# A row softmax that streams its data in equal chunks, and the same softmax on an in-place ring with a row maximum and chunks of unequal size

## The chip, the core and the metric

The kernel runs on one core of one Trainium2 chip. The core has engines that each work through their own list of instructions in order and meet through semaphores: VectorE (DVE in the profile), ScalarE (ACT), GpSimd (POOL), TensorE (PE, unused here) and SyncE (SP). Sixteen DMA engines move data between main memory and the on-chip memory; transfers are issued from the queues of SP and ACT (SPq and ACTq in the profile). The metric is the device time of one execution in microseconds. The kernel before has a median of 163.53 us over five runs (163.46 to 163.77).

## The reference: what is computed

The input has shape 16 x 1024 x 512 in float32, which is 16,384 rows of 512 numbers, 33.55 MB. Each row becomes its softmax:

```
x_max = np.max(x, axis=-1, keepdims=True)
exp_x = np.exp(x - x_max)
return (exp_x / np.sum(exp_x, axis=-1, keepdims=True)).astype(np.float32)
```

The subtraction of the row maximum cancels in the quotient. The inputs are drawn from a standard normal distribution, so an exponential without that subtraction stays small.

## The kernel before, in words

The 16,384 rows are seen as 16 chunks. One chunk has 128 partitions with R = 8 consecutive rows on each, so it is a block of 2 MB that lies together in main memory, and each partition reads or writes 16 KB of it in one piece. The loop over the chunks does the following for each.

- Load (line 47): SP issues one transfer into an `x_tile`. The pool of `x_tile` has seven buffers, so loads run far ahead of the work.
- Guard copy (line 49): GpSimd copies one column of the tile into a small tile. Nothing reads it; GpSimd just waits for each load this way. Four one-column memsets at line 80 do the same at the end for the last stores.
- Exponentials (line 61): ScalarE runs eight ACTIVATE instructions, one for each row position, from `x_tile` to `e_tile`, each 128 x 512. Each also adds up its row into a column of `sums`; that adding appears in the profile as an instruction of its own, ACTIVATION_READ_ACCUMULATOR. The row maximum is switched off (`use_max` is false), so the bias is the constant 0.
- Reciprocal (line 71) and scaling (line 74): VectorE inverts the eight sums and multiplies the whole 128 x 4096 tile by them in one TENSOR_TENSOR, in place in `e_tile`. There are four `e_tile` buffers.
- Store (line 76): ACT issues one 2 MB transfer to the output.

A scheduler orders each engine's list. On ACT it puts the sixteen exponentials of two chunks first, and then the two stores of these chunks. Completion of transfers is counted on eight semaphores, which the transfers take in turn in the order of the schedule. A transfer that takes a counter whose last user has not landed waits for it, so no more than eight transfers, loads and stores together, are under way.

The page calls a piece of a transfer that one DMA engine moves on its own a packet. Here it is the 16 KB of one partition, with small extra packets of 4 bytes that count completions.

Of the kernel before, what the change touches and what calls it, by code (L numbers as in the profile page):

```python
# [2 lines left out]

# [4 lines left out]


@with_exitstack  # L10
def kernel(
    ctx: ExitStack,
    tc: tile.TileContext,
    x: bass.AP,
    out: bass.AP,
):
    nc = tc.nc
    P = nc.NUM_PARTITIONS

    x_flat = x.flatten_outer_dims()  # L20
    out_flat = out.flatten_outer_dims()
    n, d = x_flat.shape

    R = int(os.environ.get("SM_R", "8"))
    XBUFS = int(os.environ.get("SM_XBUFS", "7"))
    EBUFS = int(os.environ.get("SM_EBUFS", "4"))

    rows_per_chunk = P * R
    assert n % rows_per_chunk == 0
    nchunks = n // rows_per_chunk  # L30

    x_t = x_flat.rearrange("(t p r) d -> t p r d", p=P, r=R)
    out_t = out_flat.rearrange("(t p r) d -> t p r d", p=P, r=R)

    x_pool = ctx.enter_context(tc.tile_pool(name="xp", bufs=XBUFS))
    e_pool = ctx.enter_context(tc.tile_pool(name="ep", bufs=EBUFS))
    stats_pool = ctx.enter_context(tc.tile_pool(name="stats", bufs=12))
    guard_pool = ctx.enter_context(tc.tile_pool(name="guard", bufs=1))

    use_max = os.environ.get("SM_USEMAX", "0") == "1"  # L40

    guard_tile = guard_pool.tile([P, 1], mybir.dt.float32)

    e_tiles = []
    for t in range(nchunks):
        x_tile = x_pool.tile([P, R, d], mybir.dt.float32)
        nc.sync.dma_start(out=x_tile, in_=x_t[t])  # L47

        nc.gpsimd.tensor_copy(out=guard_tile, in_=x_tile[:, 0, 0:1])  # L49

        if use_max:
            neg_max = stats_pool.tile([P, R], mybir.dt.float32)
            nc.vector.reduce_max(
                out=neg_max, in_=x_tile, axis=mybir.AxisListType.X, negate=True
            )

        e_tile = e_pool.tile([P, R, d], mybir.dt.float32)
        e_tiles.append(e_tile)
        sums = stats_pool.tile([P, R], mybir.dt.float32)
        for r in range(R):  # L60
            nc.scalar.activation(  # L61
                out=e_tile[:, r, :],
                in_=x_tile[:, r, :],
                func=mybir.ActivationFunctionType.Exp,
                bias=neg_max[:, r : r + 1] if use_max else 0.0,
                scale=1.0,
                accum_out=sums[:, r : r + 1],
            )

        recip = stats_pool.tile([P, R], mybir.dt.float32)  # L70
        nc.vector.reciprocal(out=recip, in_=sums)  # L71

        recip_b = recip.unsqueeze(2).to_broadcast([P, R, d])
        nc.vector.tensor_mul(out=e_tile, in0=e_tile, in1=recip_b)  # L74

        nc.scalar.dma_start(out=out_t[t], in_=e_tile)  # L76

    for b in range(min(EBUFS, nchunks)):
        e_tile = e_tiles[nchunks - 1 - b]
        nc.gpsimd.memset(e_tile[:, 0, 0:1], 0.0)  # L80


# [1 line left out]
_INS = ['x']  # L84
_OUTS = [((16, 1024, 512), 'float32')]


# [23 lines left out]
```

The softmax here doesn't subtract the row's maximum and nothing guards it: scores larger than these inputs give would overflow.

## Time and profile before

| What | Value |
|---|---|
| Median of five runs | 163.53 us |
| Profiled execution, its own time | 163.77 us |
| Its span | 161.8 us |
| VectorE busy | 74.1 us, 46% |
| ScalarE busy | 80.8 us, 50% |
| GpSimd busy | 13.5 us, 8% |
| Moved by DMA | 67.13 MB, mean 415 GB/s over the span |
| Data transfers | 16 loads and 16 stores of 2 MB |

The span runs from the first to the last instruction that the profile counts; the execution's own time is 2.0 us longer. Busy shares of engines are means over the span. The row of DMA digits on the page divides the span into 40 slices of 4.05 us and gives the mean busy share of the sixteen DMA engines in tenths. The GB/s row under it gives what they moved in the same slices. A view over chosen windows gives the same for any stretch of time; since a packet is counted where it begins, short windows swing around the true rate.

### The profile page before, as it was taken

How to read it: one execution, taken by the hardware profiler on the slowest of the kernel's cores; microseconds unless marked ns; L12 is line 12 of the kernel's file. 1: busy time of each engine (PE TensorE's matmuls, PEld its weight loads, DVE VectorE, ACT ScalarE, POOL GpSimd, SP SyncE). 2: the span in 40 equal slices, each digit the busy share in tenths (PEclk: the TensorE clock that was granted, in tenths of full speed). 3: DMA queues.
4: the chain of work that ended last, by engine and by line, in shares of the span. 5: the costliest groups of instructions: out<-in, count | busy, mean ns of one | idle time of the engine just before them, and what ended most of it. 6: DMA issues, size and time to landing. Idle time of an engine off the chain costs nothing.

```text
span 161.8 us, 456 instructions
## 1 busy us (share of the span) xinstructions
DVE 74.1 (46%) x32; ACT 80.8 (50%) x257; POOL 13.5 (8%) x24
## 2 busy tenths in 40 slices
DVE  0006960994296419082000008951992399069600
ACT  3099529924793381910000099339906980995000
POOL 0000000034080000000000006300000000000000
DMA  5999999999999999999999999999999999999993
GB/s 166 421 450 421 425 336 436 433 421 442 429 425 438 429 429 434 433 421 442 425 429 442 421 433 442 413 442 440 413 438 442 413 442 429 421 446 425 425 438 146
DMA packets 4610, 67.13 MB, mean 415 GB/s; under 512 B 512, under 2 KB 512, under 8 KB 512
## 3 DMA queue, kind: packets, MB, share of 16 engines
q1 hardware_dynamic: 2304, 33.56, 49.5%
q10 hardware_dynamic: 2304, 33.56, 48.5%
q14 instruction: 2, 0.02, 0.0%
HBM read 33.55 MB, written 33.55 MB: 415 GB/s over the span
## 4 chain that ended last, share of the span: by engine, by line
DMA 52%; ACT 28%; DVE 17%; issue 1%; ACTq 1%; POOLq 0%; SPq 0%
DMA x_tile<-in_x_dram 35%; ACT e_tile L61 28%; DMA out_dram<-e_tile 17%; DVE e_tile L74 16%; ACTq L76 1%; DVE recip L71 1%; POOLq L106 0%; POOLq L80 0%; SPq L47 0%
## 5 line engine op out<-in xcount | busy, mean ns | idle before, releaser
L61 ACT ACTIVATE e_tile<-x_tile 128x512 f32<-128x512 f32 x128 | 78.5, 615 | 66.3 <-DMA x_tile<-in_x_dram 35.2
L74 DVE TENSOR_TENSOR e_tile<-e_tile,recip 128x4096 f32<-128x4096 f32 x16 | 70.8, 4426 | 0.6
L71 DVE RECIPROCAL recip<-sums 128x8 f32<-128x8 f32 x16 | 3.2, 203 | 77.8 <-ACT e_tile L61 77.8
L61 ACT ACTIVATION_READ_ACCUMULATOR e_tile<-x_tile 128x1 f32 x128 | 23.9, 187 | 0.0
L49 POOL COPY guard_tile<-x_tile 128x1 f32<-128x1 f32 x16 | 12.9, 807 | 124.1 <-DMA x_tile<-in_x_dram 124.1
L80 POOL MEMSET e_tile<- 128x1 f32 x4 | 0.4, 99 | 23.1 <-DMA out_dram<-e_tile 23.1
L61 ACT ACT_TABLE_LOAD x1 | 1.3, 1283 | 0.7 <-PEq L95 0.7
L95 POOL MEMSET const-float32-0.0<- 128x1 f32 x1 | 0.1, 99 | 0.2 <-issue 0.2
L95 POOL MEMSET const-bfloat16-1.0<- 128x1 bf16 x1 | 0.1, 102 | 0.0
L95 POOL MEMSET const-uint8-127<- 128x1 uint8 x1 | 0.1, 102 | 0.0
L95 POOL MEMSET const-float32-1.0<- 128x1 f32 x1 | 0.1, 99 | 0.0
## 6 DMA issues: line engine op xcount, KB each, us to landing
x_tile<-in_x_dram SPq DMA_DIRECT2D x16, 2048.0 KB, 42.3
out_dram<-e_tile ACTq DMA_DIRECT2D x16, 2048.0 KB, 17.9
```

The lines of the kernel that those rows point to most:

```text
L49: nc.gpsimd.tensor_copy(out=guard_tile, in_=x_tile[:, 0, 0:1])
L61: nc.scalar.activation(out=e_tile[:, r, :], in_=x_tile[:, r, :], func=mybir.ActivationFunctionType.Exp, bias=neg_max[:, r : r + 1] if use_ ...
L71: nc.vector.reciprocal(out=recip, in_=sums)
L74: nc.vector.tensor_mul(out=e_tile, in0=e_tile, in1=recip_b)
L76: nc.scalar.dma_start(out=out_t[t], in_=e_tile)
L80: nc.gpsimd.memset(e_tile[:, 0, 0:1], 0.0)
L95: nc = _bacc.Bacc("TRN2", target_bir_lowering=False, num_devices=1)
```

## The change

The changed kernel keeps one launch, the same inputs and outputs, float32 everywhere, loads from SP and stores from ACT. It differs in these points.

- The chunks have 1, 1, 2, 4, 8, six times 16, 8, 4, 2, 1, 1 rows on each partition. That is again 16 chunks and 128 rows on each partition. The pieces that a partition moves are 2, 4, 8, 16 or 32 KB long, and a transfer has 256 KB to 4 MB.
- There is one ring of tiles. The exponentials write over the loaded data, and the scaling does too; the store reads the same tile. There are two tiles for 1-row chunks, one each for 2, 4 and 8 rows, and five for 16 rows.
- VectorE takes the negated maximum of every row (`rowmax`, one instruction for a chunk), and the exponentials use it as their bias.
- The scaling is one `tensor_scalar_mul` for each row position (128 x 512) in place of one multiplication for the chunk.
- The guard copies and the closing memsets on GpSimd are gone.
- The order on each engine is written by hand. For chunk k, VectorE takes the row maximum of k and then scales k-1; ACT runs the exponentials of k and then issues the store of k-1.

In the compiled order, the load of the sixth 16-row chunk (chunk 10, counted from 0) waits for the store of chunk 5, whose tile it takes over; the store of chunk 8 shares a completion counter with that load and waits for it to land.

```diff
+CHUNKS = [1, 1, 2, 4, 8] + [16] * 6 + [8, 4, 2, 1, 1]
+SLOTS = {1: 2, 2: 1, 4: 1, 8: 1, 16: 5}
...
-    for t in range(nchunks):
-        x_tile = x_pool.tile([P, R, d], mybir.dt.float32)
-        nc.sync.dma_start(out=x_tile, in_=x_t[t])
-        nc.gpsimd.tensor_copy(out=guard_tile, in_=x_tile[:, 0, 0:1])
+    def load(k):
+        R = CHUNKS[k]
+        tiles[k] = data.tile([P, R, d], F32, name=f"x{R}", tag=f"x{R}", bufs=SLOTS[R])
+        nc.sync.dma_start(out=tiles[k], in_=src[k])
+    def rowmax(k):
+        R = CHUNKS[k]
+        shift[k] = stats.tile([P, R], F32, name=f"shift{R}", tag=f"shift{R}")
+        nc.vector.reduce_max(out=shift[k], in_=tiles[k], axis=AX, negate=True)
...
+    def exps(k):
         for r in range(R):
             nc.scalar.activation(
-                out=e_tile[:, r, :],
-                in_=x_tile[:, r, :],
-                func=mybir.ActivationFunctionType.Exp,
-                bias=neg_max[:, r : r + 1] if use_max else 0.0,
+                out=tiles[k][:, r, :],
+                in_=tiles[k][:, r, :],
+                func=EXP,
+                bias=shift[k][:, r : r + 1],
                 scale=1.0,
-                accum_out=sums[:, r : r + 1],
+                accum_out=sums[k][:, r : r + 1],
             )
+    def scale(k):
+        nc.vector.reciprocal(out=recip, in_=sums[k])
         for r in range(R):
-        recip_b = recip.unsqueeze(2).to_broadcast([P, R, d])
-        nc.vector.tensor_mul(out=e_tile, in0=e_tile, in1=recip_b)
-        nc.scalar.dma_start(out=out_t[t], in_=e_tile)
+            nc.vector.tensor_scalar_mul(
+                out=tiles[k][:, r, :],
+                in0=tiles[k][:, r, :],
+                scalar1=recip[:, r : r + 1],
+            )
+    def store(k):
+        nc.scalar.dma_start(out=dst[k], in_=tiles[k])
-    for b in range(min(EBUFS, nchunks)):
-        e_tile = e_tiles[nchunks - 1 - b]
-        nc.gpsimd.memset(e_tile[:, 0, 0:1], 0.0)
+    with tc.manual_schedule():
+        for k in range(K):
+            load(k)
+            rowmax(k)
+            exps(k)
+            if k >= 1:
+                scale(k - 1)
+                store(k - 1)
+        scale(K - 1)
+        store(K - 1)
```

More of the change, by code (lines that the diff above doesn't have):

```diff
@@ L1 @@
-import os
 from contextlib import ExitStack
@@ L5 @@
 import concourse.tile as tile
-from concourse import bass_utils, mybir
+from concourse import mybir
 from concourse._compat import with_exitstack
+F32 = mybir.dt.float32
+EXP = mybir.ActivationFunctionType.Exp
+AX = mybir.AxisListType.X
+CHUNKS = [1, 1, 2, 4, 8] + [16] * 6 + [8, 4, 2, 1, 1]
+SLOTS = {1: 2, 2: 1, 4: 1, 8: 1, 16: 5}
 @with_exitstack
@@ L22 @@
     n, d = x_flat.shape
[L24 to L44, printed above, removed]
-    for t in range(nchunks):
-        x_tile = x_pool.tile([P, R, d], mybir.dt.float32)
-        nc.sync.dma_start(out=x_tile, in_=x_t[t])
-        nc.gpsimd.tensor_copy(out=guard_tile, in_=x_tile[:, 0, 0:1])
[L51 to L59, printed above, removed]
+    assert n == P * sum(CHUNKS)
@@ new lines @@
+    src, dst, at = [], [], 0
+    for R in CHUNKS:
+        for flat, views in ((x_flat, src), (out_flat, dst)):
+            part = flat[at : at + P * R, :]
+            views.append(part.rearrange("(p r) d -> p r d", r=R))
+        at += P * R
+    data = ctx.enter_context(tc.tile_pool(name="data", bufs=1))
+    stats = ctx.enter_context(tc.tile_pool(name="stats", bufs=4))
+    K = len(CHUNKS)
+    tiles = [None] * K
+    shift = [None] * K
+    sums = [None] * K
+    def load(k):
+        R = CHUNKS[k]
+        tiles[k] = data.tile([P, R, d], F32, name=f"x{R}", tag=f"x{R}", bufs=SLOTS[R])
+        nc.sync.dma_start(out=tiles[k], in_=src[k])
@@ L60 @@
+    def rowmax(k):
[3 more added lines that the diff above has]
+    def exps(k):
+        R = CHUNKS[k]
+        sums[k] = stats.tile([P, R], F32, name=f"sums{R}", tag=f"sums{R}")
         for r in range(R):
             nc.scalar.activation(
-                out=e_tile[:, r, :],
-                in_=x_tile[:, r, :],
-                func=mybir.ActivationFunctionType.Exp,
@@ L65 @@
-                bias=neg_max[:, r : r + 1] if use_max else 0.0,
+                out=tiles[k][:, r, :],
+                in_=tiles[k][:, r, :],
+                func=EXP,
+                bias=shift[k][:, r : r + 1],
                 scale=1.0,
-                accum_out=sums[:, r : r + 1],
+                accum_out=sums[k][:, r : r + 1],
             )
-        recip = stats_pool.tile([P, R], mybir.dt.float32)
-        nc.vector.reciprocal(out=recip, in_=sums)
-        recip_b = recip.unsqueeze(2).to_broadcast([P, R, d])
@@ L74 @@
-        nc.vector.tensor_mul(out=e_tile, in0=e_tile, in1=recip_b)
-        nc.scalar.dma_start(out=out_t[t], in_=e_tile)
-    for b in range(min(EBUFS, nchunks)):
-        e_tile = e_tiles[nchunks - 1 - b]
-        nc.gpsimd.memset(e_tile[:, 0, 0:1], 0.0)
+    def scale(k):
+        R = CHUNKS[k]
+        recip = stats.tile([P, R], F32, name=f"recip{R}", tag=f"recip{R}")
+        nc.vector.reciprocal(out=recip, in_=sums[k])
+        for r in range(R):
+            nc.vector.tensor_scalar_mul(
[3 more added lines that the diff above has]
+            )
```

## The prediction, made before the changed kernel was run

> **What bounds the kernel now.** I read the engines' busy shares first, then the row of DMA slices, then windows of DMA rate, then the instants at which transfers land, and the chain that ended last.
>
> ```profile
> DVE 74.1 (46%) x32; ACT 80.8 (50%) x257; POOL 13.5 (8%) x24
> DMA  5999999999999999999999999999999999999993
> q1 hardware_dynamic: 2304, 33.56, 49.5%
> q10 hardware_dynamic: 2304, 33.56, 48.5%
> ```
>
> No engine is busy for more than half of the span, while the DMA engines are at 90% or more in every slice but the first and the last: loads (q1) and stores (q10) together take 98.0% of 161.8 us. The windows give the rate, with the DMA share and GB/s as last columns:
>
> ```profile
> 1.70:8.00 6.30, 0.00 (x0) 0.31 (x1) 0.00 (x0) 1.00 1.01 377
> 8.00:20.00 12.00, 6.29 (x4) 9.91 (x32) 0.56 (x3) 1.00 1.01 434
> 20.00:24.00 4.00, 2.96 (x1) 0.56 (x2) 0.00 (x0) 1.00 0.96 324
> 24.00:92.00 68.00, 27.76 (x12) 29.36 (x96) 7.47 (x7) 1.00 1.01 432
> 97.00:137.00 40.00, 27.40 (x12) 25.35 (x83) 4.52 (x4) 1.00 1.01 432
> 137.00:159.00 22.00, 9.63 (x5) 9.91 (x32) 0.48 (x4) 1.00 1.00 430
> 158.00:161.00 3.00, 0.00 (x0) 0.00 (x0) 0.10 (x1) 1.00 0.38 164
> ```
>
> Loads alone (8 to 20 us), both kinds (24 to 92) and stores alone (137 to 159) all run at 430 to 434 GB/s. Three places lose something: the start, the window in which the first store begins (20 to 24 us, 324 in place of 432: (432-324)/432 x 4 = 1.0 us), and the last 3 us. The closing memsets on GpSimd, each released by a store, show the landings:
>
> ```profile
> 146.37 0.10 POOL L80 MEMSET e_tile<- 128x1 f32 x1 [8.88 <-DMA out_dram<-e_tile]
> 151.19 0.10 POOL L80 MEMSET e_tile<- 128x1 f32 x1 [4.73 <-DMA out_dram<-e_tile]
> 156.04 0.10 POOL L80 MEMSET e_tile<- 128x1 f32 x1 [4.74 <-DMA out_dram<-e_tile]
> 160.90 0.10 POOL L80 MEMSET e_tile<- 128x1 f32 x1 [4.76 <-DMA out_dram<-e_tile]
> ```
>
> The last four stores land 4.84 us apart, 8 rows each: 0.607 us to move one row on every partition one way (a "row" below), and 128 rows in plus 128 out are 256 x 0.607 = 155.4 us. The chain of waits names ACT and DVE for 45% of the span, but these are steps beside a full DMA stream: its last link is the store that lands at 160.76.
>
> **The change, part by part.** The sum is made against the profiled execution, 163.77 us (span 161.8), which is 0.24 above the median.
>
> ```profile
> L61 ACT ACTIVATE e_tile<-x_tile 128x512 f32<-128x512 f32 x128 | 78.5, 615 | 66.3 <-DMA x_tile<-in_x_dram 35.2
> L61 ACT ACTIVATION_READ_ACCUMULATOR e_tile<-x_tile 128x1 f32 x128 | 23.9, 187 | 0.0
> L74 DVE TENSOR_TENSOR e_tile<-e_tile,recip 128x4096 f32<-128x4096 f32 x16 | 70.8, 4426 | 0.6
> L71 DVE RECIPROCAL recip<-sums 128x8 f32<-128x8 f32 x16 | 3.2, 203 | 77.8 <-ACT e_tile L61 77.8
> ```
>
> *Bytes and descriptors.* Still 16 loads and 16 stores with 128 data descriptors each and the same bytes. Whatever part of a descriptor's 0.607 us is fixed and whatever part goes by bytes, the sum stays 155.4 us; I take 0. It fails only if time is not a straight line in size. No row shows another size. Below: 16-row pieces (192 of the 256 rows, 116.5 us) 1% faster give -1.2. Above: the 2 to 8 KB pieces (32 rows, 19.4 us) at half the rate give +19.4. I stay by the 16 KB row.
>
> *Short transfers.* Twelve transfers are 256 or 512 KB. On a queue with work waiting, 2 MB takes 4.84 us, which is 433 GB/s with nothing between transfers, so I charge 0 as long as the next transfer is queued. The Trainium skill ("DMA: Bandwidth & Descriptors", § Rules for kernel authors and § Anatomy of one DMA) speaks against them: at least 1 MiB for each DMA, and about 2.0 us fixed for each. By it 2 MB would be 6.8 us, which the 4.84 contradicts for queued transfers; by it the sum would be +24 us for the twelve if none overlapped.
>
> *GpSimd.* 16 copies and 4 memsets go. Only the last memset ends the chain (160.76 to 161.0): -0.2 at most; SP waits for the stores in its place. I take -0.1.
>
> *VectorE.* Row maximum: 128 rows. TENSOR_TENSOR does 8 rows in 4.426, so 0.553 a row, 70.8 us; from the difference of the two DVE rows, (4426-203)/4088 = 1.03 ns per element and 0.19 us fixed, so 8.7 us for 16 rows. Scaling: 128 instructions on 128x512, a form not shown. Ends: 0.20 (RECIPROCAL, nearly all fixed) and 0.72 (0.19 + 512 x 1.03 ns). It reads one stream like the first and 512 elements like the second; I take the middle, 0.46. Sum 70.8 + 58.9 + 3.2 = 133 us (100 to 166), against 74.1. For a 16-row chunk: 8.7 + 7.4 + 0.2 = 16.3 us (12 to 20.4), beside 32 x 0.607 = 19.4 us of DMA. It hides, except near the upper end. The Trainium skill ("VectorE: DVE Perf Modes", § The perf-mode tier table) lets float32 tensor_scalar run at two elements per cycle, an estimate of 0.33 us, and tensor_reduce only at one; by it VectorE would be busy 116 us and the sum the same.
>
> *ScalarE.* The bias becomes a column of a tile. Today eight exponentials take 4.91 us, 0.614 each. Ends: 0.614, and 0.80 (615 + 187, nothing overlapped); I take 0.71, the middle: 11.4 us for 16 rows, 91 in all. Hidden behind the 19.4 of DMA.
>
> *Order and ring.* Store k-1 now stands behind the exponentials of k, which wait for load k and its row maximum. That costs only where the DMA engines have nothing else, so I follow their backlog. The first load took 7.60 us to land, 4.86 of it data, so 2.7 us is start and receipt. The ring takes 96 rows of loads before any waits for a store.
>
> Start: loads alone, as now; compute lags, but loads fill the stream. Load 5 lands near 25 us; VectorE then does rowmax 5, scale 4, rowmax 6 (to 47), the exponentials of 6 end near 58.5, and store 5 is issued. Sharing evenly with loads it lands near 83. By then (83-2-1)/0.607 = 132 rows have moved: 96 loads and 36 stores, so loads 0 to 9 are just done and store 6, issued near 75, keeps the stream full.
>
> Chunk 10, the narrow place: its load is issued at 83.2 and lands at 83.2 + 2.7 + 32 x 0.607 = 105.3. By then 168.6 rows have moved, 112 in and 56.6 out. Chunks 0 to 7 are 64 rows, so 7.4 are left, plus store 8 (16, released by this landing), plus loads 11 to 15 (16): 39.4 rows, work until 129.2. Store 9 needs rowmax 10 (8.7) and exponentials 10 (11.4), so it is issued at 105.3 + 0.5 + 20.1 = 125.9 and moves data by 128.6 at the latest. It is covered by 0.6 us.
>
> End: 48 rows of stores remain from 129.2, 29 us. VectorE's rest is scale 10 (7.4) and chunks 11 to 15 (16 x 1.01 + 1 = 17): done near 151, ahead of the stream's end. The last 1-row store has no computing left in front of it.
>
> Sum: DMA 0, engines 0, GpSimd -0.1, nothing exposed: 163.7, against a median of 163.53.
>
> **The rivals.**
> *Gap at chunk 10.* With 0.80 us an exponential, the cover of 0.6 turns into a gap of 0.8; a load 10 that waits two more 32 KB packets per engine (2.4 us) for its turn lets stores eat as much of the cover, giving 2 to 3. For it: the thin margin. Against it: 2.7 us was the dearest start in the trace and is counted twice. It decides once row maximum, exponentials and start together exceed 23.9 us. Price 0.4 to 3: 164.1 to 166.7.
> *Descriptor size matters.* 2 to 8 KB pieces 5 to 20% dearer: 19.4 us x that = 1 to 4 us: 164.7 to 167.7. Against it: none of the three mixes in the trace changed the rate.
> *VectorE becomes the bound.* Above about 0.53 for a scaling (16 x 0.53 + 8.9 passes the cover at chunk 10) every hundredth adds about 1 us: 0.6 gives some 170.
> *The start gets cheaper.* The 1.0 us dip with the first store, and the last 3 us in which engines finish apart (164 GB/s: 1.9 us of work missing), may shrink when the first and last transfers are small: -0.5 to -1.5, so 162.2 to 163.2. Against it: nothing says the dip goes by size.
> *32 KB pieces may not be made.* If they are cut into 16 KB ones, the rate is today's and the time too.
>
> **How the numbers follow.** A measurement of this kernel can tell about 0.2%, 0.33 us. Unbroken stream 0.45, own range 163.1 to 164.3 (0.32 same, 0.08 slower, 0.05 faster); gap 0.22, descriptors 0.12, VectorE 0.05, all slower; cheaper start 0.16, faster. That is faster 0.21, same 0.32, slower 0.47. I predict 163.7; from 162.6 to 166.4 leaves out VectorE, the upper half of the descriptors' case and the edges of two others, under 0.2.
>
> **What the profile of the changed kernel would show.** Right: DMA digits of 9 throughout, 430 to 434 GB/s, about 4,610 packets, VectorE busy near 116 to 133 us, ScalarE near 90. A digit under 9 between 125 and 132 us is the gap. Lower GB/s in the first 10 us and at the end is descriptor size. VectorE without idle time from 60 us on is the third. The prediction is wrong if the stream has other limits than bytes.

## The result and the profile after

The changed kernel took 165.11 us (median of 21 executions, 163.78 to 167.03), and the kernel before, run beside it, 163.57 us (41 executions, 163.35 to 164.08). The ratio is 1.0086, with a 95% interval of 1.0069 to 1.0104: about 1.4 to 1.5 us slower. Three executions lie over 1.5% above the fastest; the ratio leaves them out. The profiled execution of the changed kernel took 164.15 us, with a span of 162.4. It lies near the fast end of its kernel's executions, so its trace can show only some 0.4 us of the loss against the 163.77 of the profiled execution before.

From the page of the changed kernel (busy time of the engines, share and instructions; the DMA engines' busy tenths and GB/s in 40 slices of 4.06 us; the packets):

```profile
DVE 124.4 (77%) x160; ACT 93.1 (57%) x257; POOL 0.2 (0%) x4
DMA  6999999999999999999999999999999998998993
GB/s 159 367 407 440 446 445 437 436 402 414 454 430 428 418 440 452 420 460 412 428 452 412 436 452 398 408 452 432 436 402 454 462 443 364 465 458 382 411 384 142
DMA packets 4611, 67.14 MB, mean 413 GB/s; under 512 B 512, under 2 KB 512, under 8 KB 2048
```

VectorE works 124.4 us in place of 74.1, and it still doesn't set the time: the DMA row is full until the 33rd slice. The 4,611 packets say that nothing was cut up: as many pieces moved as before. Windows of the changed kernel (from:to, length, busy time and instructions of DVE, ACT and POOL, TensorE clock, DMA share, GB/s):

```profile
1.70:10.00 8.30, 3.58 (x7) 3.15 (x6) 0.00 (x0) 1.00 1.01 346
1.70:24.00 22.30, 13.22 (x17) 10.23 (x26) 0.00 (x0) 1.00 1.02 402
24.00:120.00 96.00, 86.55 (x97) 64.69 (x183) 0.00 (x0) 1.00 1.00 431
157.00:162.00 5.00, 1.89 (x5) 0.81 (x2) 0.00 (x0) 1.00 0.51 198
```

The same windows of the kernel before:

```profile
1.70:10.00 8.30, 0.00 (x0) 1.95 (x6) 0.18 (x1) 1.00 1.00 385
1.70:24.00 22.30, 9.26 (x4) 10.79 (x35) 0.56 (x3) 1.00 1.00 398
24.00:120.00 96.00, 43.97 (x20) 49.18 (x160) 11.99 (x11) 1.00 1.01 431
157.00:162.00 5.00, 0.00 (x0) 0.00 (x0) 0.10 (x1) 1.00 0.41 174
```

In the middle both move 431 GB/s. In the first 10 us the changed kernel moves 346 instead of 385, which is (385 - 346) / 431 x 8.3 = 0.75 us of work. The DMA share of 1.01 (1.00 before) says that the engines were no more idle there; their pieces took longer than usual (those of 4 KB 0.24 us on average, 0.16 as a rule). By 24 us the changed kernel has caught up (402 against 398): it doesn't have the dip that the kernel before has with its first store (435 GB/s from 10 to 24 us, 406 before). If the bytes of each piece are spread over its own time in the packet records, both kernels have moved the same 66.1 of 67.1 MB by 157 us. The last piece ends at 160.43 us in the kernel before and at 161.22 in the changed one. So this execution loses some 0.8 us, all of it at the end. The timeline of the changed kernel shows why the end is thin (start and length in us, engine, line, operation; in brackets how long the engine had been idle and what released it):

```profile
143.91 1.22 DVE L57 TENSOR_REDUCE shift<-x 128x2 f32<-128x1024 f32 x1 [5.13 <-DMA x<-in_x_dram]
...
152.30 0.69 DVE L57 TENSOR_REDUCE shift<-x 128x1 f32<-128x512 f32 x1 [5.38 <-DMA x<-in_x_dram]
...
157.23 0.69 DVE L57 TENSOR_REDUCE shift<-x 128x1 f32<-128x512 f32 x1 [3.26 <-DMA x<-in_x_dram]
...
158.54 0.34 ACTq L84 DMA_DIRECT2D out_dram<-x  x1
159.52 0.34 ACTq L84 DMA_DIRECT2D out_dram<-x  x1
```

VectorE has nothing to do and waits for loads. The loads of 2, 1 and 1 rows land at 143.9, 152.3 and 157.2 us: a load of 256 KB takes 8.4 us after the one before it, though its data is 0.6 us of work. Loads and stores take turns at each DMA engine piece by piece: between 143.9 and 152.3 us the packet records have 143 load pieces of 2 KB and 143 store pieces, 92 of 16 KB and 51 of 32 KB. A piece of 2 KB takes 0.084 us, one of 16 KB 0.61 and one of 32 KB 1.21. Each DMA engine moves eight pieces of a small load. Alternating with this mix of store pieces they take 8 x (0.08 + 0.83) = 7.3 us, and with 32 KB pieces alone 8 x (0.08 + 1.21) = 10.3; the 8.4 lies between. The last two stores are issued when little else is left to move.

### The profile page after: what moved, and what is told of

Read it like the earlier page. It is cut to its first block, busy times and chain, and to the rows that moved or that the text cites. A ratio compares the mean times of both kernels' runs of the same rounds, so it can differ in the third digit from the quotient of the medians.

```text
span 162.4 us, 523 instructions
## 1 busy us (share of the span) xinstructions
DVE 124.4 (77%) x160; ACT 93.1 (57%) x257; POOL 0.2 (0%) x4
## 2 busy tenths in 40 slices
DMA packets 4611, 67.14 MB, mean 413 GB/s; under 512 B 512, under 2 KB 512, under 8 KB 2048
## 4 chain that ended last, share of the span: by engine, by line
DMA 46%; DVE 29%; ACT 12%; another core or an unknown queue 8%; SPq 1%; issue 1%; ACTq 0%
DMA x<-in_x_dram 29%; DVE shift L57 18%; DMA out_dram<-x 17%; ACT x L63 12%; DVE x L77 10%; SPq L52 1%; DVE recip L75 1%; ACTq L84 0%; ACTq L63 0%
## 5 line engine op out<-in xcount | busy, mean ns | idle before, releaser
L63 ACT ACTIVATE x<-x,shift 128x512 f32<-128x512 f32 x128 | 90.5, 709 | 62.2 <-DVE shift L57 56.9
L57 DVE TENSOR_REDUCE shift<-x 128x16 f32<-128x8192 f32 (+4 forms) x16 | 70.7, 4417 | 32.9 <-DMA x<-in_x_dram 32.8
L77 DVE TENSOR_SCALAR x<-x,recip 128x512 f32<-128x512 f32 x128 | 52.1, 481 | 0.6
L63 ACT ACTIVATION_READ_ACCUMULATOR x<-x,shift 128x1 f32 x128 | 24.0, 187 | 0.0
L75 DVE RECIPROCAL recip<-sums 128x16 f32<-128x16 f32 (+4 forms) x16 | 3.1, 195 | 1.6 <-ACT x L63 1.6
```

The costliest lines, as they stand in the source:

```text
L57: nc.vector.reduce_max(out=shift[k], in_=tiles[k], axis=AX, negate=True)
L63: nc.scalar.activation(out=tiles[k][:, r, :], in_=tiles[k][:, r, :], func=EXP, bias=shift[k][:, r : r + 1], scale=1.0, accum_out=sums[k][: ...
L75: nc.vector.reciprocal(out=recip, in_=sums[k])
L77: nc.vector.tensor_scalar_mul(out=tiles[k][:, r, :], in0=tiles[k][:, r, :], scalar1=recip[:, r : r + 1],)
```

## The experiments

Times are medians. Each ratio is to the kernel before, run on the same chip in the same job (163.50 to 163.65). Diffs are against the changed kernel. The first question was which of three things costs: the small chunks at the end, the small chunks at the start, or the rest (ring, row maximum, order).

**The last two loads issued early**

```diff
-SLOTS = {1: 2, 2: 1, 4: 1, 8: 1, 16: 5}
+SLOTS = {1: 4, 2: 1, 4: 1, 8: 1, 16: 5}
-            load(k)
+            if k < 14:
+                load(k)
+            if k == 4:
+                load(14)
+                load(15)
```

> The changed kernel with one move: the loads of the last two 1-row chunks (14 and 15) are issued right after load 4, into two tiles of their own; work and order on VectorE and ScalarE stay. In the changed kernel load 15 lands near 157.2 us of the span, and row maximum, exponential, scaling and store issue of a single row then stand alone until 159.5. Theory of the tail (the last small loads take turns with long store pieces, land too late, and the last row's chain runs with the DMA engines idle): 163.3 to 163.8, and the spread of over 3 us between runs (163.78 to 167.03) shrinks under 1 us. Rival of the start (the small first transfers cost the time): nothing changes, about 165.1 with the same spread. Rival of the ring and the row maximum: about 165.1 too.

Measured: 164.40 us, ratio 1.0048 (1.0036 to 1.0060). Its timeline at the end:

```profile
147.84 0.68 DVE L57 TENSOR_REDUCE shift<-x 128x1 f32<-128x512 f32 x1
...
149.42 0.68 DVE L57 TENSOR_REDUCE shift<-x 128x1 f32<-128x512 f32 x1
...
151.70 0.34 ACTq L84 DMA_DIRECT2D out_dram<-x  x1
```

The last two row maxima no longer wait for a load, and the last store is issued 7.8 us earlier. That is worth 0.7 us (165.11 to 164.40); about the same again is left over, more than the 163.3 to 163.8 that the end alone would leave, so the end is not the whole cause. The spread between executions did shrink as expected, from over 3 us to 0.4 (164.24 to 164.64, five executions). The start of this trace is the worst of all: 326 GB/s from 1.7 to 10 us.

**The ring with equal chunks**

```diff
-CHUNKS = [1, 1, 2, 4, 8] + [16] * 6 + [8, 4, 2, 1, 1]
-SLOTS = {1: 2, 2: 1, 4: 1, 8: 1, 16: 5}
+CHUNKS = [8] * 16
+SLOTS = {8: 12}
```

> The changed kernel with sixteen chunks of 8 rows and a ring of twelve tiles of 16 KB per partition: ring, row maximum, scaling by rows and hand-written order stay, only the sizes go back. Theory of the tail: 163.3 to 163.8 with under 1 us of spread, since load 15 lands long before the stores end. Rival of the start: the same 163.5, as the small first transfers are gone too. Rival of the ring and the row maximum (their work costs the time, whatever the sizes): 164.5 to 166.

Measured: 163.20 us, ratio 0.9976 (0.9964 to 0.9987). Ring, row maximum, hand-written order, 128 scalings and the missing guard copies together cost nothing; they gain 0.4 us. All of the loss, about 1.9 us from 163.20 to 165.11, comes with the sizes of the chunks.

**No small chunks at the start**

```diff
-CHUNKS = [1, 1, 2, 4, 8] + [16] * 6 + [8, 4, 2, 1, 1]
+CHUNKS = [16] * 7 + [8, 4, 2, 1, 1]
```

> The changed kernel with its first five chunks (1, 1, 2, 4, 8) replaced by one of 16; the end 8, 4, 2, 1, 1 stays. Theory of the tail: the late small loads remain, so 164.5 to 166 and a spread of some us remain. Rival of the start: 163.3 to 163.8. If the later first store leaves the DMA engines idle, a DMA digit under 9 in the first half of the span would show it and the time says nothing on either.

Measured: 163.79 us, ratio 1.0014 (1.0002 to 1.0027). The same end, large chunks at the start: 1.3 us better. The window of its start:

```profile
1.70:10.00 8.30, 0.00 (x0) 0.00 (x0) 0.00 (x0) 1.00 1.07 430
```

430 GB/s, in place of 346. Part of that is the counting: a piece counts where it begins, and sixteen pieces of 32 KB across the window's end are 63 GB/s in 8.3 us (the share of 1.07 shows it). With the bytes spread over each piece's own time it is 386, against 329 in the changed kernel and 373 in the kernel before. That contradicts a theory of the end alone.

**No row maximum**

```diff
-                bias=shift[k][:, r : r + 1],
+                bias=0.0,
...
-            rowmax(k)
```

> The changed kernel without the row maximum: the bias is the constant 0, so VectorE loses 70.7 us and the exponentials start as soon as a load lands. (Left out: the subtraction of the maximum.) Theory of the tail: the last row's chain loses 0.7 us of row maximum and 0.1 of the exponential, the late landing of load 15 stays: 164.2 to 164.8 and still a spread of us. Rival of the ring and the row maximum: 163.5. Rival of the start: 165.1.

Measured: 164.81 us, ratio 1.0070 (1.0047 to 1.0094). From its page:

```profile
DVE 55.4 (34%) x144; ACT 81.3 (50%) x257; POOL 0.2 (0%) x4
```

And from its timeline at the end:

```profile
154.23 0.63 ACT L63 ACTIVATE x<-x 128x512 f32<-128x512 f32 x1 [6.66 <-DMA x<-in_x_dram]
...
158.56 0.63 ACT L63 ACTIVATE x<-x 128x512 f32<-128x512 f32 x1 [3.61 <-DMA x<-in_x_dram]
```

VectorE loses 69 us of work, and the time hardly moves. Now it is ScalarE that waits for the last loads, as late as before. The row maximum is not the cause, not even of the thin end.

**Small chunks at the start alone, on a ring of 8 rows**

```diff
-CHUNKS = [1, 1, 2, 4, 8] + [16] * 6 + [8, 4, 2, 1, 1]
-SLOTS = {1: 2, 2: 1, 4: 1, 8: 1, 16: 5}
+CHUNKS = [1, 1, 2, 4, 8] + [8] * 14
+SLOTS = {1: 2, 2: 1, 4: 1, 8: 11}
```

> The equal ring (sixteen chunks of 8 rows, 163.20) with only its first 16 rows cut as in the changed kernel: 1, 1, 2, 4, 8, then fourteen chunks of 8; eleven 16 KB tiles. No small chunk at the end. If the small first transfers cost time by themselves: 164.0 to 164.6, and less than 400 GB/s between 1.7 and 24 us of the span, where the equal ring has 413 and the kernel with the last two loads moved forward has 382. If the small start only costs together with long pieces or a small end: 163.1 to 163.5.

Measured: 164.83 us, ratio 1.0057 (1.0037 to 1.0077); seven executions from 163.67 to 164.92. With 16-row chunks and the small end both gone, the small start alone costs 164.83 - 163.20 = 1.6 us by the medians, and 1.3 by the two ratios (1.0057 and 0.9976). The profiled execution is the fastest of the seven (163.67), so its trace shows only a part of this.

**A start of two 4-row chunks**

```diff
-CHUNKS = [1, 1, 2, 4, 8] + [16] * 6 + [8, 4, 2, 1, 1]
-SLOTS = {1: 2, 2: 1, 4: 1, 8: 1, 16: 5}
+CHUNKS = [4, 4] + [8] * 15
+SLOTS = {4: 2, 8: 11}
```

> The equal ring with its first chunk cut in two of 4 rows. If any first transfer that is shorter than 2 MB starves the DMA engines: 163.7 to 164.2. If it takes the 256 and 512 KB ones: 163.1 to 163.5.

Measured: 163.08 us, ratio 0.9968 (0.9955 to 0.9980), the fastest of all, 0.5 us ahead of the kernel before. Two transfers of 1 MB at the front do no harm: 401 GB/s from 1.7 to 10 us.

**Large chunks throughout**

```diff
-CHUNKS = [1, 1, 2, 4, 8] + [16] * 6 + [8, 4, 2, 1, 1]
-SLOTS = {1: 2, 2: 1, 4: 1, 8: 1, 16: 5}
+CHUNKS = [16] * 7 + [8, 8]
+SLOTS = {16: 5, 8: 2}
```

> The changed kernel with chunks of 16 rows seven times and then 8 and 8, five tiles of 32 KB and two of 16 KB per partition: neither a small start nor small last loads. Head and tail together explain the loss: 162.6 to 163.2, at or below the equal ring, since long pieces at the start gave 423 GB/s between 1.7 and 24 us. If 32 KB pieces cost time themselves: 163.6 or more. If the last two chunks of 8 rows come too late, a DMA digit under 9 in the last fifth of the span shows it, with 164 or more.

Measured: 163.47 us, ratio 0.9995 (0.9980 to 1.0010), twelve executions from 162.84 to 164.45. That lies between the two expectations. Without any small chunk the 16-row ring is level with the kernel before, 0.3 us behind the ring of 8 rows and less steady from one execution to the next.

**Pieces of 2 KB in transfers of 2 MB**

```diff
-CHUNKS = [1, 1, 2, 4, 8] + [16] * 6 + [8, 4, 2, 1, 1]
-SLOTS = {1: 2, 2: 1, 4: 1, 8: 1, 16: 5}
+CHUNKS = [8] * 16
+SLOTS = {8: 12}
...
-            views.append(part.rearrange("(p r) d -> p r d", r=R))
+            views.append(part.rearrange("(r p) d -> p r d", r=R))
```

> The equal ring, with the rows of a chunk given to the partitions in another order, so that every transfer still has 2 MB but moves it in pieces of 2 KB in place of 16 KB: eight times as many data descriptors. It prices the size of a piece alone. If the time goes by bytes only: 163.2. If 16 KB takes 607 ns of which some 5 ns are fixed, 2 KB takes 80 and the sum grows by 5%: 170 to 173. If small pieces are limited by something dearer: 180 and up.

Measured: 174.52 us, ratio 1.0661 (1.0639 to 1.0683). Its packets by the page:

```profile
DMA packets 33283, 67.14 MB, mean 390 GB/s; under 512 B 512, under 2 KB 512, under 8 KB 33280
```

A window of its middle:

```profile
40.00:120.00 80.00, 62.01 (x81) 45.67 (x129) 0.00 (x0) 1.00 1.05 407
```

The size of a piece has a price when there are more of them: 407 GB/s in place of 431. Each of the 16 DMA engines moves 2,048 data pieces in place of 256, and the 163.20 of the equal ring becomes 174.52: 11.3 us / 1,792 = 6.3 ns for each further piece. By the rates of the middle alone it is less: 67.1 MB take 9.2 us longer at 407 than at 431 GB/s, 5.1 ns for a piece. The rest was lost at the start (363 GB/s from 1.7 to 24 us, 413 in the equal ring). So the fixed part of a piece is some 5 to 6 ns. Since the changed kernel has as many pieces as the kernel before, the size of its pieces in itself costs it nothing.

**The small chunks behind one large load**

This is the kernel with the small start on the ring of 8 rows, with the first 8-row load issued ahead of the four small ones. The order of the computing is the same.

```diff
-CHUNKS = [1, 1, 2, 4, 8] + [16] * 6 + [8, 4, 2, 1, 1]
-SLOTS = {1: 2, 2: 1, 4: 1, 8: 1, 16: 5}
+CHUNKS = [1, 1, 2, 4, 8] + [8] * 14
+SLOTS = {1: 2, 2: 1, 4: 1, 8: 11}
...
+        for k in (4, 0, 1, 2, 3):
+            load(k)
         for k in range(K):
-            load(k)
+            if k > 4:
+                load(k)
```

> The kernel with the small start on the equal ring (1, 1, 2, 4, 8, then fourteen 8s; 164.83 with 163.67 to 164.92), and only the order of its first five loads changed: the 2 MB load of chunk 4 goes first, then 0, 1, 2, 3. Sizes, pieces and the order of the computing stay; the first row is computed some 5 us later. If the small transfers cost because they are the first ones and run out before the next are there: 163.0 to 163.5, and between 1.7 and 10 us of the span 380 GB/s or more in place of 359. If small pieces cost wherever they stand: still 164.3 to 164.9.

Measured: 163.17 us, ratio 0.9980 (0.9971 to 0.9989), twelve executions from 163.04 to 163.50. The same transfers, only in another order: 164.83 becomes 163.17. This is the cleanest pair of the study. Small transfers behind a large one are free, the same ones in front cost 1.6 us (1.3 by the ratios). The windows of the start, first without the move and then with it:

```profile
1.70:10.00 8.30, 3.96 (x8) 4.32 (x9) 0.00 (x0) 1.00 0.96 359
1.70:10.00 8.30, 0.83 (x2) 0.79 (x1) 0.00 (x0) 1.00 1.00 369
```

The time came as expected, the rate did not: 369 GB/s, not 380 or more. The two profiled executions (163.67 and 163.04) are only 0.6 us apart, so the traces show less than half of the effect. That the DMA engines lack a queue with work in it is one reading (their share is 0.96 without the move and 1.00 with it). Another stands beside it: the new order also issues the first store later, at 12.07 us in place of 6.48, and in the changed kernel the pieces are slow and the engines no more idle than before. No run took the two apart.

**The sizes of the changed kernel, with loads moved at both ends**

```diff
-SLOTS = {1: 2, 2: 1, 4: 1, 8: 1, 16: 5}
+SLOTS = {1: 4, 2: 1, 4: 1, 8: 1, 16: 5}
...
+        for k in (4, 0, 1, 2, 3, 14, 15):
+            load(k)
         for k in range(K):
-            load(k)
+            if 4 < k < 14:
+                load(k)
```

> The changed kernel with all its chunk sizes, and only loads moved: the 2 MB load of chunk 4 goes first, then 0 to 3, then the last two 1-row loads 14 and 15 (two more 1-row tiles), then the rest in order. Head and tail together explain the whole loss by where the small loads stand, not by their size: 163.1 to 163.6, against 164.40 with the last two loads moved alone and 165.11 without either. If sizes matter beyond that (long pieces taking turns, unequal DMA engines): 164 or more.

Measured: 164.96 us, ratio 1.0079 (1.0066 to 1.0093): a miss. The start is mended (409 GB/s from 1.7 to 24 us, 382 where only the last loads were moved), and the last loads are early, but there is a new loss in the middle. From its timeline, the issue of loads 10 to 13 and the row maximum that waited for load 10:

```profile
83.34 4.48 SPq L52 DMA_DIRECT2D x<-in_x_dram  x4
...
110.15 8.69 DVE L57 TENSOR_REDUCE shift<-x 128x16 f32<-128x8192 f32 x1 [11.86 <-DMA x<-in_x_dram]
```

Load 10 is issued at 83.3, when its tile comes free, and in the trace load 9 has landed at about 72: the load queue stood empty, and the load took 27 us. The slowest stretch lies behind that restart:

```profile
96.00:102.00 6.00, 2.30 (x6) 6.00 (x19) 0.00 (x0) 1.00 0.92 345
```

In this window (431 - 345) / 431 x 6 = 1.2 us is lost. By bytes spread over each piece's own time about 1.2 us are lost between 80 and 100 us together, in two places: near 87 us, where the loads start again, and near 97 us, where the store queue has run empty (the next store is issued at 98.95); there a 32 KB piece takes up to 2.7 us in place of 1.21. Which of the two queues costs the time isn't shown. The kernel without the row maximum has such a stretch too, 382 GB/s between 96 and 102 us.

**Both ends small and moved, without 16-row chunks**

```diff
-CHUNKS = [1, 1, 2, 4, 8] + [16] * 6 + [8, 4, 2, 1, 1]
-SLOTS = {1: 2, 2: 1, 4: 1, 8: 1, 16: 5}
+CHUNKS = [1, 1, 2, 4, 8] + [8] * 13 + [4, 2, 1, 1]
+SLOTS = {1: 4, 2: 1, 4: 1, 8: 11}
...
+        for k in (4, 0, 1, 2, 3, 20, 21):
+            load(k)
         for k in range(K):
-            load(k)
+            if 4 < k < 20:
+                load(k)
```

> Chunks 1, 1, 2, 4, 8, then thirteen of 8, then 4, 2, 1, 1 rows, on a ring of eleven 8-row tiles, with the loads of the first 8-row chunk issued ahead of the first small ones and those of the last two 1-row chunks right behind the small head. It has the small transfers at both ends, moved as in the run that kept the sizes of the changed kernel (164.96 us), but no 16-row transfer. If what was left in that run comes from the ring of five 16-row tiles, whose load queue ran empty for some 15 us and restarted slowly: 163.0 to 163.5, as the 8-row rings with and without a small head gave 163.1 to 163.2, and 90 to 120 us at 431 GB/s. If it comes from small transfers at the end in themselves, whenever their loads are issued: 164.2 or more, with the last five microseconds under 240 GB/s.

Measured: 163.84 us, ratio 1.0020 (1.0012 to 1.0029), eleven executions from 163.74 to 164.18. The window in which the kernel before this one lost most:

```profile
96.00:102.00 6.00, 4.42 (x1) 0.00 (x0) 0.00 (x0) 1.00 1.01 434
```

434 GB/s in place of 345, and the time falls by 1.1 us: without the 16-row ring the loss in the middle is gone. The result still lies between the two expectations. Against the 163.17 with small chunks at the start alone, a small end costs 0.7 us even with its last two loads moved. These six further transfers are 48 pieces for each DMA engine, by the 5 to 6 ns above 0.3 us; but the 48 further pieces by which the 163.17 kernel exceeds the equal ring did not show, so this split stays open.

**A small end alone, nothing moved**

```diff
-CHUNKS = [1, 1, 2, 4, 8] + [16] * 6 + [8, 4, 2, 1, 1]
-SLOTS = {1: 2, 2: 1, 4: 1, 8: 1, 16: 5}
+CHUNKS = [8] * 15 + [4, 2, 1, 1]
+SLOTS = {1: 2, 2: 1, 4: 1, 8: 11}
```

> Fifteen chunks of 8 rows and then 4, 2, 1 and 1, loads in the order of the chunks, ring of eleven 8-row tiles: the small tail alone, nothing moved, behind 16 KB store pieces in place of 32 KB ones. The equal ring took 163.20 us. If a small load waits eight turns of a store piece (8 x 0.61 us here, 8 x 1.21 us behind 32 KB pieces), the last four loads land some 4 to 6 us apart, the last store is issued before 155 us, and the time is 163.2 to 163.7. If a small tail costs its price whatever stands before it (0.7 to 1.3 us, from the run that moved the last loads and from the profile of the changed kernel): 163.9 to 164.5.

Measured: 167.91 us, ratio 1.0267 (1.0253 to 1.0281). Neither theory. The DMA row of its page:

```profile
DMA  5999999999999999999999999999999998928996
```

Three lines of its timeline, the stores of chunks 6 and 7 and an exponential behind the second:

```profile
87.32 0.34 ACTq L84 DMA_DIRECT2D out_dram<-x  x1
...
106.81 0.34 ACTq L84 DMA_DIRECT2D out_dram<-x  x1
107.28 0.72 ACT L63 ACTIVATE x<-x,shift 128x512 f32<-128x512 f32 x1 [13.77 <-DMA x<-in_x_dram]
```

The store of chunk 7 is issued at 106.81. In the equal ring it comes at 93.44:

```profile
87.31 0.34 ACTq L84 DMA_DIRECT2D out_dram<-x  x1
...
93.44 0.34 ACTq L84 DMA_DIRECT2D out_dram<-x  x1
```

In the compiled order three more chunks have shifted the turn of the completion counters. Here store 7 waits on the counter of a later load (chunk 13); in the equal ring it waits on that of load 11. It is ahead of exponentials on ACT that were ready to run: the row maximum of their chunk ended at 101.4. VectorE then works without a break to the end and the stores come too late, so the DMA engines run dry at about 145 us (the digit 2). This kernel says nothing about the price of a small end. That the counter is the cause is read from the semaphore that store 7 waits for, which is that of chunk 13's load, and from the issue times; no run took it away by itself. The ring also has eleven tiles in place of twelve, as in the kernels with the small start, which show no such loss.

## Why the prediction was right in part and wrong in the rest

The range of 162.6 to 166.4 held the 165.11, and "slower" had the largest chance of the three signs. That is luck: the upper part of the range was priced for a gap at chunk 10 and for dearer descriptors, and neither came. But the likeliest case was an unbroken stream at 163.7, and the measured median lies outside that case's own range of 163.1 to 164.3. The loss came by none of the rivals. The sum also set out from the profiled execution, 163.77, and was held against the median of 163.53; from the median it gives 163.4.

*What held.*
- **Bytes and descriptors** at 0: 431 GB/s in the middle of both, and by the 2 KB run a piece costs a fixed 5 to 6 ns plus its bytes, close to a straight line. The rival that descriptor size matters fell with this; it would matter only with more pieces. Its sign, lower GB/s in the first 10 us, did appear (346 against 385), so the sign couldn't tell this rival from small transfers in front.
- **VectorE** was taken as 8.7 us for a 16-row maximum, and the trace has 8.69 to 8.70. A scaling was taken as 0.46 us; sixteen in a row take 6.22 us, so 0.39 each. That puts the busy time at 124.4, between the 133 by the rows and the 116 by the page "VectorE: DVE Perf Modes" of the Trainium skill (§ The perf-mode tier table), from which 0.33 us was estimated: the two-at-a-time rate is there in part. VectorE was never the bound.
- **ScalarE** was taken as 0.71 us for an exponential; they follow each other every 0.705 us.
- **Order and ring**, in the middle. From the chain that ended last in the changed kernel:

```profile
54.95 27.29 DMA out_dram<-x
82.26 0.03 SPq L52
82.29 0.05 issue
82.33 23.91 DMA x<-in_x_dram
106.27 8.70 DVE shift L57
```

Store 5 was put at 58.5 to 83 us and load 10 at 83.2 to 105.3; the chain has 55.0 to 82.2 and 82.3 to 106.2. The gap at chunk 10 did not open. The cover was wider than the 0.6 us worked out, because store 9 was issued at 122.29 and not at 125.9: four microseconds before the exponentials of chunk 10, which precede it in ACT's list, had ended.
- The **32 KB pieces** were made (192 rows in them, and no more packets than before).

*What failed.*
- **Short transfers**: "I charge 0 as long as the next transfer is queued". Behind a large load the 0 held (163.17 against 163.20). I didn't ask where the condition fails: at the start nothing is queued yet. The term there is 1.3 us (165.11 to 163.79 by a large start) to 1.6 us (164.83 to 163.17 by order alone). The Trainium skill's "DMA: Bandwidth & Descriptors" (§ Rules for kernel authors, at least 1 MiB for each DMA) points at the right transfers here: those of 256 and 512 KB in front cost, two of 1 MB in front did not. As a price for each transfer its 2.0 us fixed (§ Anatomy of one DMA, which gives it for transfers issued from GpSimd; here SP and ACT issue them) does not show: behind one large load the same four small ones cost nothing measurable.
- **Order and ring**, at the end: "The last 1-row store has no computing left in front of it", with VectorE done near 151 us. I shared the DMA engines between loads and stores by bytes. They share by pieces (143 to 143 above): a short load has as many pieces as a long store and waits for one of them at every turn. So the last loads landed at 152.3 and 157.2 us and the last store was issued at 159.5. Early last loads bring 0.7 us.
- **The start gets cheaper**, the rival in the other direction, had its sign wrong for small chunks in front. The dip with the first store is gone in the profiled execution of the changed kernel (437 GB/s from 20 to 24 us in place of 324), but the first 10 us lost as much; in the equal ring the dip comes later (369 GB/s from 24 to 28 us). The order and the ring did bring a little, 0.4 us in the equal ring, against the 0.1 that I took from GpSimd; what part of the change brings it wasn't separated.

The sum by these terms is 163.20 + 1.3 to 1.6 (start) + 0.7 (end) = 165.2 to 165.5, against 165.11 measured. The 1.3 and the 0.7 are themselves differences from the 165.11, so this is a check that the terms fit together and no proof. The kernel with loads moved at both ends doesn't bear the sum out: it took 164.96, with a new loss in the middle.

*What stays open.* The profiled execution of the changed kernel doesn't show the loss at the start: up to 40 us it is level with the equal ring (415 and 414 GB/s from 1.7 us on), and what it loses it loses at the end. The run with early last loads, profiled at its median, has 405, which is (414 - 405) / 431 x 38.3 = 0.8 us. So the term of the start rests on the medians of the kernels that differ in it; what makes the pieces slow there isn't shown. Nor is it settled why the kernels with small chunks at the start, or with late small loads behind 32 KB stores, spread so differently: over 3 us in the changed kernel, 2.7 without the row maximum, 1.3 with the small start on the ring of 8 rows, but 0.4 with the last loads early. The 16-row ring without small chunks spread over 1.6 us (162.84 to 164.45), rings of 8 rows without small chunks in front over 0.2 to 0.5.

## What to carry to other kernels

Where the DMA engines are the bound, ask of every small transfer what stands in its queue before it and what takes turns with it. Small loads belong behind a large one, not in front; small loads at the end belong early, because beside a stream of long pieces they cost turns and not bytes. After a change in the number of transfers, look again at which completion counter each of them waits on: three more chunks came with one store issued 13 us later and a kernel 4.7 us slower.

## What the runs showed of the hardware that was not expected

- Loads and stores take turns piece by piece whatever their length (143 load pieces of 2 KB to 143 store pieces of 16 and 32 KB): 256 KB beside 32 KB pieces took 8.4 us, 4.9 us when the stores had shrunk.
- A piece has a fixed cost of some 5 to 6 ns on its DMA engine (1,792 more pieces, 9.2 us by the rates of the middle, 11.3 us in all).
- Four transfers of 256 KB to 1 MB cost 1.3 to 1.6 us at the front of an empty queue and nothing measurable behind a 2 MB load.
- A load queue that stood empty for some ten microseconds beside a busy store queue was followed by a stretch of 345 GB/s in place of 431, in which the store queue ran empty too. It was gone in the kernel with shorter tiles; milder forms between 96 and 102 us are in the kernel without the row maximum (382 GB/s) and in the changed kernel (406).
- ACT issued a store 4 us before exponentials ahead of it in its list had ended.
